# Additions of weight blocks in DRAM: placed under later products, and two blocks summed in place of three

## The chip, the cores and the metric

The kernel is one program on one core of a Trainium2 chip. The metric is the device time of an execution in microseconds, as the median of several runs. A core has five engines with an instruction queue each, which it works off in order: TensorE (PE, matrix products, with its weight loads as PEld), VectorE (DVE), ScalarE (ACT), GpSimd (POOL) and SyncE (SP). An engine whose next instruction waits for a semaphore does nothing of what stands behind it. Transfers are issued on the queues of SP, ACT and POOL and run beside the engines.

## The reference

One decoder block on 256 tokens of width 2048, in float32. What matters here are the stages and their order:

```python
u = rmsnorm(h, norm1_g[l])
proj = u @ w_in[l]                                   # 16896 columns
hq, hf, hi, hg, aq, ak, av, gate_a, gate_b = split(proj)
ya = hgrn2_branch(hq, hf, hi, hg, ...) @ w_proj_a[l]
yb = dilated_attention_branch(aq, ak, av) @ w_proj_b[l]
mix = sigmoid(gate_a) * ya + sigmoid(gate_b) * yb
h = h + mix @ w_out[l]
v = rmsnorm(h, norm2_g[l])
h = h + conv_ffn(v, w_up[l], conv_w[l], conv_b[l], w_down[l])
out = rmsnorm(h, norm_f_g)
```

The attention rotates q and k (`x1*cos - x2*sin`, `x2*cos + x1*sin`), and adds a mask to its scores.

## The kernel before

**The stream of weights.** All matrices are read once, as 300 units of 16 blocks of 128x128 (1 MB each), in the order in which they are multiplied: units 0 to 35 are the attention's columns, 36 to 99 HGRN's, 100 to 131 the gates', 132 to 167 the two projections and the output product, and from 168 on the up and down products of the feed-forward part, in eleven blocks b of 512 hidden columns. SP loads a unit into one of three tiles `raw` (L291). ScalarE rounds it to a high part (L368), VectorE forms the low part (L369), both called hl, and TensorE multiplies high and low parts separately (three matmuls for a product). `begin_unit` splits two units ahead and loads three ahead. So VectorE's hl operations are on the way of everything that TensorE does.

**Units of kind S.** In the up product most pairs of row blocks use seven products in place of eight (`PRODUCTS["S"]`), with sums of weight blocks. A unit holds b11, b21, b22 and b12, each 128x512. There are 49 such units. One of the sums is made in DRAM long before (`add_blocks`, L245): SP copies b12 into a DRAM tile q (L255), then POOL adds b11 (L256) and b22 (L257) to it with accumulating transfers. Each of the two waits on POOL until the one before it has landed. `begin_unit` spreads these 49 sums over the units from ADD_FROM = 20 on, ADD_SPAN = 140 units long. When the unit is loaded, three of its blocks come from the weights (L287) and the fourth is q (L288). `split_s` then makes the parts sa (b11, b21), se (b22 and the sum), sf (two more sums) and sg (one more), with three additions or subtractions on VectorE (L339, L340, L342).

**What else is on POOL.** The rotation of q and k needs the two halves of the head swapped, for which POOL issues two transfers each (L632, L633, tiles xs_q and xs_k). VectorE multiplies them with the sines (L638) and adds them (L640). POOL also loads the masks (L676, L677) and the table `lev` of HGRN's levels (L737), which ScalarE turns into seven masks `cu` (L741). While HGRN's first products (z0p) run, the attention's scores (sc), exponentials (L704), normalisation (L708) and transposes (tr, L715) are mixed in.

**PSUM banks.** The seven sums of a block lie in banks 1 to 7. `unfold` combines them: it reads p1 and p6 first (L597, L598), then p7 and p2 (L605, L607), p5 twice (L608, L609), p4 and p3 (L610, L611). The two down products of a block follow directly (tiles dn, L525 to L527), one with banks 1 and 6, the other with 4 and 5. A matmul into a bank waits until `unfold` has read it.

**What sets the order.** Apart from the first products and SP's additions, which are tied to a place, a scheduler in the compiler arranges each engine's instructions by its own estimate of times.

Of the kernel before, what the change touches and what calls it, by code (L numbers as in the profile page):

```python
# [11 lines left out]
F32 = mybir.dt.float32  # L12
# [3 lines left out]
ALU = mybir.AluOpType  # L16
AX = mybir.AxisListType

P = 128
# [12 lines left out]
FB = 4  # L32
# [19 lines left out]
def up_modes(b):  # L52

    return "PPPSSPSP" if b < 3 else UP_PAIRS
# [5 lines left out]
def up_order(b):  # L60


    return {0: (0, 1, 2, 5, 3, 7, 4, 6), 1: (0, 1, 2, 3, 5, 4, 6, 7), 2: (0, 1, 2, 3, 5, 4, 6, 7)}.get(b, tuple(range(KD // 2)))
# [66 lines left out]
NUNITS = len(stream_spec()[0]) // UNIT  # L130
MODES = stream_spec()[1]
ADDS = sum(mode == "S" for mode in MODES.values())
ADD_FROM, ADD_SPAN = 20, 140

# [49 lines left out]
def hybrid_block(ctx, tc, x_p, x_t, weights, g1, gf, params, c_rope, c_mask0, c_mask1, c_level, out):  # L186
    nc = tc.nc
    vec, act, pe = nc.vector, nc.scalar, nc.tensor
# [16 lines left out]
    def stage(name):  # L205
        return late["stage"].tile([P, 512], F32, tag="o2", name=name, bufs=6 if "pool" in late else STAGES - 2)
# [4 lines left out]
    def e4(shape, name):  # L211
        return sbe.tile([P] + list(shape), F32, tag="e4", name=name, bufs=4)
# [4 lines left out]
    def bank(i, name):  # L217
        return ps8.tile([P, 512], F32, tag=f"b{i}", name=name)

    def main_bank(name):  # L220
        turn[0] += 1
        return bank((turn[0] - 1) % 4, name)
# [20 lines left out]
    raws, splits, late = {}, {}, {}  # L243
    dram = ctx.enter_context(tc.tile_pool(name="dram", bufs=1, space=bass.MemoryType.DRAM))
    loaded, ready, to_add = [], {}, deque(sorted(u for u, mode in MODES.items() if mode == "S"))  # L245

    def add_blocks():

        if not to_add:
            return  # L250
        u = to_add.popleft()
        ready[u] = q = dram.tile([P, 512], F32, tag=f"q2_{u}", name=f"q2_{u}")
        b = [weights[u, :, i * 512 : (i + 1) * 512] for i in range(4)]
        with in_turn(loaded[-1]):
            nc.sync.dma_start(q, b[3])  # L255
        nc.gpsimd.dma_start(q, b[0], accum_op=ALU.add)  # L256
        nc.gpsimd.dma_start(q, b[2], accum_op=ALU.add)  # L257

    ring = [0]
    last = [None, None]  # L260
# [1 line left out]
    @contextmanager  # L262
    def in_turn(*instructions):

        with ExitStack() as stack:
            for i in instructions:
                stack.enter_context(tc.issue_after(i.ins))
            yield
# [44 lines left out]
    def two_parts(hi, lo, src):  # L313

        act.activation(hi, src, AF.Copy)  # L315
        vec.tensor_tensor(lo, src, hi.bitcast(F32), op=ALU.subtract)  # L316

    def pair_tile(name):

        more = late.get("pool")  # L320
        n = ring[0] % (6 if more else 4)
        ring[0] = (n + 1) if more else (n + 1) % 4
        pool, bufs = (wp, 4) if n < 4 else (more, 2)
        return pool.tile([P, 2, 1024], F32R, tag="pair", name=name, bufs=bufs)

    def split_s(u):

        r = raws[u].rearrange("p (b n) -> p b n", b=4)
        pool = late["pool"]

        def parts(name, src):
            t = pair_tile(name)
            hi, lo = t[:, 0].rearrange("p (b n) -> p b n", b=2), t[:, 1].rearrange("p (b n) -> p b n", b=2)
            two_parts(hi, lo, src)
            return [(hi[:, i], lo[:, i]) for i in range(2)]

        b11, b21 = parts(f"sa{u}", r[:, 0:2])
        b22, q2 = parts(f"se{u}", r[:, 2:4])
        vec.tensor_tensor(r[:, 0], r[:, 3], r[:, 0], op=ALU.subtract)  # L339
        vec.tensor_tensor(r[:, 1], r[:, 3], r[:, 1], op=ALU.add)  # L340
        q3, q4 = parts(f"sf{u}", r[:, 0:2])
        vec.tensor_tensor(r[:, 3], r[:, 3], r[:, 2], op=ALU.subtract)  # L342
        g = pool.tile([P, 2, 512], F32R, tag="sg", name=f"sg{u}", bufs=1)
        two_parts(g[:, 0], g[:, 1], r[:, 3])
        splits[u] = {"11": b11, "21": b21, "22": b22, "q3": q3, "q2": q2, "q4": q4, "q1": (g[:, 0], g[:, 1])}

    def split(u):
        if u >= NUNITS or u in splits:
# [36 lines left out]
    def pump(us):  # L385
        debt[0] += us
        while side and debt[0] > 0:
            try:
                debt[0] -= next(side[0])
            except StopIteration:  # L390
                side.popleft()
        if not side:
            debt[0] = min(debt[0], 0.0)

    def drain():
        while side:
            for _ in side[0]:
                pass
            side.popleft()
        debt[0] = 0.0  # L400

    def begin_unit(u):
        for v in range(u, u + LOOKAHEAD + 1):
            split(v)
        load(u + LOOKAHEAD + 1)
        pump(SIDE_US)
        if u >= ADD_FROM and (u - ADD_FROM) * ADDS // ADD_SPAN < ADDS:
            while len(to_add) > ADDS - 1 - (u - ADD_FROM) * ADDS // ADD_SPAN:
                add_blocks()
# [110 lines left out]
    def moving_step(pst, parts, k, k0, nk):  # L520

        hi, lo = next_tiles(4)
        for m in range(2):
            xh, xl = parts(k, m)
            pe.matmul(pst[m], xl, hi, start=(k == k0), stop=False)  # L525
            pe.matmul(pst[m], xh, hi, start=False, stop=False)  # L526
            pe.matmul(pst[m], xh, lo, start=False, stop=(k == k0 + nk - 1))  # L527

    def moving(parts, k0, nk, name, pst=None):

        pst = pst or [main_bank(f"{name}_{m}") for m in range(2)]
        for k in range(k0, k0 + nk):
            moving_step(pst, parts, k, k0, nk)
        return pst
# [2 lines left out]


    PRODUCTS = {
        "S": ((1, "a11", "11"), (2, "a12", "21"), (6, "x2", "q2"), (3, "x4", "22"), (7, "x3", "q3"), (4, "a22", "q4"), (5, "x1", "q1")),  # L540
        "P": (
            (2, "a11", "11"), (2, "a12", "21"), (4, "a21", "11"), (4, "a22", "21"),
            (5, "a21", "12"), (5, "a22", "22"), (3, "d1", "12"), (3, "d2", "22"),
# [32 lines left out]
    def sevenfold(ops, modes_of, order, name):  # L576

        sums = {i: late_bank(i, f"{name}_{i}") for i in range(1, 8)}
        left = {i: sum(p[0] == i for mode in modes_of for p in PRODUCTS[mode]) for i in sums}
        fresh = set(sums)  # L580
        for i in order:
            w = next_pair()
            for b, x, n in PRODUCTS[modes_of[i]]:
                (xh, xl), (wh, wl) = ops[i][x], w[n]
                left[b] -= 1
                pe.matmul(sums[b], xl, wh, start=b in fresh, stop=False)  # L586
                pe.matmul(sums[b], xh, wh, start=False, stop=False)  # L587
                pe.matmul(sums[b], xh, wl, start=False, stop=left[b] == 0)  # L588
                fresh.discard(b)
        return sums  # L590
# [269 lines left out]
    def four(name, by_half=False):  # L860

        t = e4([2, HG, P], name) if name[0] == "q" else w4([2, HG, P] if by_half else [HG, T], name)
        for h in range(HG):
            ps = stationary(x_pair, KD, f"{name}p{h}")
            if by_half:
                second = w1(f"{name}t{h}")
                act.activation(second, ps[:, T:], AF.Copy)
                vec.tensor_tensor(t[:, :, h], halves(ps[:, :T]), halves(second), op=ALU.add)
            else:
                summed(ps, t[:, h], f"{name}t{h}")  # L870
        if by_half:
            r = halves(rstd)[:, :, None, :].to_broadcast([P, 2, HG, P])
        else:
            r = rstd[:, None, :].to_broadcast([P, HG, T])
        vec.tensor_tensor(t, t, r, op=ALU.mult)
        return t
# [6 lines left out]
    for g in range(NGRP):  # L883
        z = four(f"z{g}", True)
        f = e4([2, HG, P], f"f{g}")
        act.activation(f, z, AF.Sigmoid)
        act.activation(z, z, AF.Sigmoid, scale=-1.0)
        for h in range(HG):
            i = g * HG + h
            vec.tensor_scalar(f[:, :, h], f[:, :, h], lb[:, 1, i : i + 1], lb[:, 0, i : i + 1], op0=ALU.mult, op1=ALU.add)  # L890
            vec.tensor_scalar(z[:, :, h], z[:, :, h], lb[:, 1, i : i + 1], None, op0=ALU.mult)
        q = four(f"q{g}", True)
# [4 lines left out]
        pst = moving(x_parts, 0, KD, f"gp{g}")  # L897
# [79 lines left out]
    for j in range(NJ):  # L977
        pst = moving(mix_parts, 0, KD, f"wo{j}")
# [23 lines left out]
    def late_bank(i, name):  # L1002
        return bank(place[i], name)
# [50 lines left out]
    for b in range(NBLK):  # L1054
        sums = sevenfold(hv, up_modes(b), up_order(b), f"up{b}")
        drain()
        side.append(hidden_side(b, sums))
        pump(0.0001)
        for j, b0, b1 in DOWN.get(b, ()):
            pst = moving(ff_parts, b0 * FB, (b1 - b0) * FB, f"dn{b}_{j}", [late_bank(i, f"dn{b}_{j}_{i}") for i in ((4, 5) if j % 2 else (1, 6))])  # L1060
            for m in range(2):
                if b == NBLK - 1:
                    vec.tensor_tensor(ht[j][:, m], ht[j][:, m], pst[m], op=ALU.add)
                else:
                    t = stage(f"dns{b}_{j}_{m}")
                    act.activation(t, pst[m], AF.Copy)  # L1066
                    nc.gpsimd.dma_start(ht[j][:, m], t, accum_op=ALU.add)  # L1067
# [9 lines left out]
    for m in range(2):  # L1077
# [16 lines left out]
        v, r, t = v3[:, mc], r3[:, mc], s3[:, mc]  # L1094
# [57 lines left out]
```

## Time and profile before

| what | us |
|---|---|
| runs: median (lowest to highest of 3) | 1750.25 (1747.96 to 1752.4) |
| the profiled execution | 1752.61 |
| its span, first to last instruction | 1750.8 |
| mean granted TensorE clock | 0.994 |

| stage by the trace, us from the start | PE busy | clock | DMA share |
|---|---|---|---|
| 100 to 150 | 50.00 of 50 | 1.00 | 0.74 |
| 150 to 200 | 48.55 of 50 | 1.00 | 0.83 |
| 200 to 250 | 32.47 of 50 | 0.83 | 0.57 |
| 400 to 500 | 100.00 of 100 | 1.00 | 0.70 |
| 1700 to 1751 | 42.50 of 51 | 0.97 | 0.28 |

In the rows of a profile "L369" is the line of the kernel, and "hl<-raw" the tiles written and read, without their numbers. A row of the timeline gives the start, the duration, and in brackets how long the engine had been idle before it and what ended that. The granted clock is the share of full speed that TensorE was allowed. A matmul's duration (0.39) overlaps the next one; the starts lie 0.23 apart.

### The profile page before, as it was taken

To read this page: it belongs to the slowest core of one execution; us is meant where nothing else is said; L and a number is where in the kernel's file an instruction comes from. 1 tells how busy PE (TensorE), PEld (TensorE's weight loads), DVE (VectorE), ACT (ScalarE), POOL (GpSimd) and SP (SyncE) were. 2 spreads that over 40 slices of the span, in tenths; PEclk is the share of its full clock that TensorE was granted. 3 is DMA by queue.
4 is the path that set the end of the run, shared out by engine and by line. 5 is a ranking of instruction groups with operands and counts; after the bars stand their busy time and mean duration, and the time that the engine had idled before them with its cause. 6 is when DMAs were issued, how large, how long until landed. Compare 5 with 4: busy or idle time off the path is not lost.

```text
span 1750.8 us, 21856 instructions
## 1 busy us (share of the span) xinstructions
PE 1720.1 (98%) x8325; PEld 1441.0 (82%) x8325; DVE 1299.6 (74%) x1562; ACT 1035.4 (59%) x1414; POOL 120.5 (7%) x159
## 2 busy tenths in 40 slices
PE   9999879999999999999999999999999999999998
PEld 7888768888888888888888888788888888888886
DVE  7665547586867766544565678899999989989986
ACT  6444346555555454544443667778777776776773
POOL 0001110000000010001010000000000000000000
PEclk9999989999999999999999999999999999999999
DMA  7668755767776776688887756656666566566562
GB/s 276 230 209 248 199 171 163 221 216 204 216 216 211 217 219 213 209 247 229 279 255 233 222 170 215 214 194 201 222 227 220 188 229 228 176 233 235 185 253 96
DMA packets 81785, 376.05 MB, mean 215 GB/s; under 512 B 9312, under 2 KB 9568, under 8 KB 49808
## 3 DMA queue, kind: packets, MB, share of 16 engines
q1 hardware_dynamic: 59616, 330.87, 52.7%
q0 software_dynamic: 20768, 40.38, 14.2%
q10 hardware_dynamic: 1296, 3.41, 0.5%
q8 instruction: 65, 1.06, 0.2%
q14 instruction: 40, 0.33, 0.1%
HBM read 359.94 MB, written 40.63 MB: 229 GB/s over the span
## 4 chain that ended last, share of the span: by engine, by line
PE 87%; issue 6%; DMA 4%; DVE 2%; ACT 1%; SPq 0%; POOL 0%; DVEq 0%; ACTq 0%; POOLq 0%
PE up L586 7%; PE up L588 7%; PE up L587 7%; PE dn L525 4%; PE dn L527 4%; PE dn L526 4%; PE egp L526 3%; PE egp L525 3%; PE egp L527 3%; DMA q<-weights 2%; PE aq L438 2%; PE ak L438 2%; PE gp L525 2%; PE wo L525 2%; PE gp L527 2%
## 5 line engine op out<-in xcount | busy, mean ns | idle before, releaser
L368 ACT ACTIVATE hl<-raw 128x1024 fp32r<-128x1024 f32 (+1 forms) x502 | 526.0, 1055 | 520.3 <-PE egp L527 79.4
L369 DVE TENSOR_TENSOR hl<-raw,hl 128x1024 fp32r<-128x1024 f32 (+1 forms) x502 | 605.5, 1219 | 303.9 <-ACT hl L368 301.8
L525 PE MATMUL dn<-hl,ff 128*128 128x512 f32 x320 | 127.2, 397 | 0.0
L527 PE MATMUL dn<-hl,ff 128*128 128x512 f32 x320 | 124.9, 390 | 0.0
L526 PE MATMUL dn<-hl,ff 128*128 128x512 f32 x320 | 124.7, 390 | 0.0
L525 PE MATMUL egp<-hl,xu 128*128 128x512 f32 x256 | 100.5, 393 | 0.0
L527 PE MATMUL egp<-hl,xu 128*128 128x512 f32 x256 | 99.8, 390 | 0.0
L526 PE MATMUL egp<-hl,xu 128*128 128x512 f32 x256 | 99.7, 389 | 0.0
L315 ACT ACTIVATE sf<-raw 128x1024 fp32r<-128x1024 f32 x49 | 52.3, 1067 | 69.3 <-DVE raw L340 69.0
L586 PE MATMUL up<-hl,hva 128*128 128x512 f32 x198 | 77.3, 390 | 0.0
L587 PE MATMUL up<-hl,hva 128*128 128x512 f32 x198 | 77.2, 390 | 0.0
L588 PE MATMUL up<-hl,hva 128*128 128x512 f32 x198 | 77.1, 389 | 0.0
L256 POOL DMA_DIRECT2D q<-weights x49 | 40.1, 818 | 501.4 <-DMA q<-weights 501.4
L1067 POOL DMA_DIRECT2D h<-dns x36 | 31.1, 917 | 617.8 <-ACT dns L1066 610.8
L527 PEld LDWEIGHTS dn<-hl,ff 128*128 128x128 f32 x320 | 60.1, 188 | 12.9
L525 PEld LDWEIGHTS dn<-hl,ff 128*128 128x128 f32 x320 | 60.1, 188 | 11.7
L526 PEld LDWEIGHTS dn<-hl,ff 128*128 128x128 f32 x320 | 60.2, 188 | 11.6
L438 PE MATMUL ak<-xu,hl 128*128 128x512 f32 x192 | 68.0, 399 | 0.0
L316 DVE TENSOR_TENSOR se<-raw,se 128x1024 fp32r<-128x1024 f32 x49 | 59.8, 1221 | 9.6 <-ACT se L315 9.6
L316 DVE TENSOR_TENSOR sf<-raw,sf 128x1024 fp32r<-128x1024 f32 x49 | 59.9, 1222 | 9.0 <-ACT sf L315 9.0
L316 DVE TENSOR_TENSOR sa<-raw,sa 128x1024 fp32r<-128x1024 f32 x49 | 59.8, 1221 | 4.5 <-ACT sa L315 3.7
L315 ACT ACTIVATE sa<-raw 128x1024 fp32r<-128x1024 f32 x49 | 52.0, 1062 | 14.6 <-PE up L588 6.6
(587 smaller groups left out, 4420.2 us busy)
## 6 DMA issues: line engine op xcount, KB each, us to landing
raw<-weights SPq DMA_DIRECT2D x249, 1024.0 KB, 5.3
raw<-weights SPq DMA_DIRECT2D x49, 768.0 KB, 4.3
q<-weights POOLq DMA_DIRECT2D x98, 256.0 KB, 6.4
q<-weights SPq DMA_DIRECT2D x49, 256.0 KB, 5.6
raw<-q SPq DMA_DIRECT2D x49, 256.0 KB, 4.6
h<-dns POOLq DMA_DIRECT2D x36, 256.0 KB, 3.8
h<-x_t ACTq DMA_DIRECT2D x4, 512.0 KB, 5.7
xt<-x_p SPq DMA_DIRECT2D x3, 512.0 KB, 10.0
```

What stands on the lines that cost most here:

```text
L256: nc.gpsimd.dma_start(q, b[0], accum_op=ALU.add)
L315: act.activation(hi, src, AF.Copy)
L316: vec.tensor_tensor(lo, src, hi.bitcast(F32), op=ALU.subtract)
L368: last[0] = act.activation(hi[:, q * w : (q + 1) * w], raw, AF.Copy)
L369: last[1] = vec.tensor_tensor(lo[:, q * w : (q + 1) * w], raw, hi[:, q * w : (q + 1) * w].bitcast(F32), op=ALU.subtract)
L438: pe.matmul(ps, hi, pair, start=(k == 0), stop=False, skip_group_check=True)
L525: pe.matmul(pst[m], xl, hi, start=(k == k0), stop=False)
L526: pe.matmul(pst[m], xh, hi, start=False, stop=False)
L527: pe.matmul(pst[m], xh, lo, start=False, stop=(k == k0 + nk - 1))
L586: pe.matmul(sums[b], xl, wh, start=b in fresh, stop=False)
L587: pe.matmul(sums[b], xh, wh, start=False, stop=False)
L588: pe.matmul(sums[b], xh, wl, start=False, stop=left[b] == 0)
```

## The change

Three things. The sums in DRAM begin at unit 44 in place of 20 and are spread over 120 units. Each adds b11 to b12 only; the sum with b22 is now made on VectorE, first of the three operations, in a tile q of its own. Which sum comes from DRAM thereby changes from q2 to q1, and with it the place of products 5 and 6 in the row of seven, and the banks of the down products.

```diff
-ADD_FROM, ADD_SPAN = 20, 140
+ADD_FROM, ADD_SPAN = 44, 120
...
-        ready[u] = q = dram.tile([P, 512], F32, tag=f"q2_{u}", name=f"q2_{u}")
+        ready[u] = q = dram.tile([P, 512], F32, tag=f"q1_{u}", name=f"q1_{u}")
         b = [weights[u, :, i * 512 : (i + 1) * 512] for i in range(4)]
         with in_turn(loaded[-1]):
             nc.sync.dma_start(q, b[3])
         nc.gpsimd.dma_start(q, b[0], accum_op=ALU.add)
-        nc.gpsimd.dma_start(q, b[2], accum_op=ALU.add)
...
         b11, b21 = parts(f"sa{u}", r[:, 0:2])
-        b22, q2 = parts(f"se{u}", r[:, 2:4])
-        vec.tensor_tensor(r[:, 0], r[:, 3], r[:, 0], op=ALU.subtract)
-        vec.tensor_tensor(r[:, 1], r[:, 3], r[:, 1], op=ALU.add)
+        q2 = pool.tile([P, 512], F32, tag="q", name=f"q{u}", bufs=1)
+        vec.tensor_tensor(q2, r[:, 2], r[:, 3], op=ALU.add)
+        b22, q1 = parts(f"se{u}", r[:, 2:4])
+        vec.tensor_tensor(r[:, 0], q2, r[:, 0], op=ALU.subtract)
+        vec.tensor_tensor(r[:, 1], q2, r[:, 1], op=ALU.add)
         q3, q4 = parts(f"sf{u}", r[:, 0:2])
-        vec.tensor_tensor(r[:, 3], r[:, 3], r[:, 2], op=ALU.subtract)
         g = pool.tile([P, 2, 512], F32R, tag="sg", name=f"sg{u}", bufs=1)
-        two_parts(g[:, 0], g[:, 1], r[:, 3])
+        two_parts(g[:, 0], g[:, 1], q2)
...
-        "S": ((1, "a11", "11"), (2, "a12", "21"), (6, "x2", "q2"), (3, "x4", "22"), (7, "x3", "q3"), (4, "a22", "q4"), (5, "x1", "q1")),
+        "S": ((1, "a11", "11"), (2, "a12", "21"), (5, "x1", "q1"), (3, "x4", "22"), (7, "x3", "q3"), (4, "a22", "q4"), (6, "x2", "q2")),
...
-[late_bank(i, f"dn{b}_{j}_{i}") for i in ((4, 5) if j % 2 else (1, 6))]
+[late_bank(i, f"dn{b}_{j}_{i}") for i in ((4, 6) if j % 2 else (1, 5))]
```

On POOL, at the end of the attention's products, stood before (q2_181 and the like are the sums in DRAM by their units, xs_k2 the last swap):

```order
L256 DMA q2_181_1634<-weights 128x512
L632 DMA xs_k2_1629<-akraw2_1430 64x1024
L633 DMA xs_k2_1629<-akraw2_1430 64x1024
L257 DMA q2_181_1634<-weights 128x512
L256 DMA q2_182_1735<-weights 128x512
L676 DMA mask0_1765<-c_mask0 128x384
L257 DMA q2_182_1735<-weights 128x512
L677 DMA mask1_1766<-c_mask1 128x768
L737 DMA lev_1771<-c_level 128x896
```

And there stands now:

```order
L632 DMA xs_k2_1613<-akraw2_1418 64x1024
L633 DMA xs_k2_1613<-akraw2_1418 64x1024
L676 DMA mask0_1741<-c_mask0 128x384
L677 DMA mask1_1742<-c_mask1 128x768
L737 DMA lev_1747<-c_level 128x896
L256 DMA q1_172_2347<-weights 128x512
L256 DMA q1_174_2482<-weights 128x512
```

Six units' additions stood ahead of the levels; the first of all 49 now stands behind them. On VectorE, at the last two swaps of k, the sum L640 also moved: it now follows L638 directly, with the hl that stood between them behind it.

On VectorE a unit of kind S in the feed-forward part (unit 238; raw238 is its tile) read before:

```order
L316 TENSOR_TENSOR sa238_10950<-raw238_10926,sa238_10950 128x1024
L316 TENSOR_TENSOR se238_10953<-raw238_10926,se238_10953 128x1024
L339 TENSOR_TENSOR raw238_10926<-raw238_10926 128x512
L340 TENSOR_TENSOR raw238_10926<-raw238_10926 128x512
L342 TENSOR_TENSOR raw238_10926<-raw238_10926 128x512
L316 TENSOR_TENSOR sf238_10958<-raw238_10926,sf238_10958 128x1024
L316 TENSOR_TENSOR sg238_10962<-raw238_10926,sg238_10962 128x512
```

And now (lines between the two places of the diff have moved up by one):

```order
L315 TENSOR_TENSOR sa238_10929<-raw238_10905,sa238_10929 128x1024
L338 TENSOR_TENSOR q238_10932<-raw238_10905 128x512
L315 TENSOR_TENSOR se238_10934<-raw238_10905,se238_10934 128x1024
L340 TENSOR_TENSOR raw238_10905<-q238_10932,raw238_10905 128x512
L341 TENSOR_TENSOR raw238_10905<-q238_10932,raw238_10905 128x512
L315 TENSOR_TENSOR sg238_10942<-q238_10932,sg238_10942 128x512
L315 TENSOR_TENSOR sf238_10939<-raw238_10905,sf238_10939 128x1024
```

The sum has moved ahead of se, and sg no longer reads the raw tile. In some other units L338 stands ahead of sa, or one hl of the unit before it.

On TensorE, at the end of block 6's up product (the third part of a name is the bank), stood before:

```order
L588 MATMUL up6_3_10783<-hl239_1_10991,hvd7_7899 128x512
L525 MATMUL dn6_2_1_11098<-hl240_0_11020,ff3_0_9794 128x512
L526 MATMUL dn6_2_1_11098<-hl240_0_11020,ff3_0_9794 128x512
L527 MATMUL dn6_2_1_11098<-hl240_0_11020,ff3_0_9794 128x512
L525 MATMUL dn6_2_6_11099<-hl240_0_11020,ff3_0_9794 128x512
```

And now:

```order
L588 MATMUL up6_3_10760<-hl239_1_10971,hvd7_7850 128x512
L525 MATMUL dn6_2_1_11078<-hl240_0_11000,ff3_0_9762 128x512
L526 MATMUL dn6_2_1_11078<-hl240_0_11000,ff3_0_9762 128x512
L527 MATMUL dn6_2_1_11078<-hl240_0_11000,ff3_0_9762 128x512
L525 MATMUL dn6_2_5_11079<-hl240_0_11000,ff3_0_9762 128x512
```

The first matmul into the second bank waits for another read of `unfold`. In other blocks the scheduler has pulled more matmuls into bank 1 ahead of the first into bank 5: eleven in blocks 2, 4 and 10, nine in block 3, six in block 5, three in blocks 6 to 9. In block 1 all of the first bank's and a bank of the second product come first. Behind block 0, which has no down product, 20 matmuls now stand ahead of the first into bank 5: 18 into bank 2, and two of unit 179's sg into bank 6, pulled ahead of two whole units. On VectorE stand until L609 there: L598, two hl around it, L605, L338 of unit 179, L608.

More of the change, by code (lines that the diff above doesn't have):

```diff
@@ L337, in split_s @@
         b11, b21 = parts(f"sa{u}", r[:, 0:2])
-        b22, q2 = parts(f"se{u}", r[:, 2:4])
-        vec.tensor_tensor(r[:, 0], r[:, 3], r[:, 0], op=ALU.subtract)
-        vec.tensor_tensor(r[:, 1], r[:, 3], r[:, 1], op=ALU.add)
+        q2 = pool.tile([P, 512], F32, tag="q", name=f"q{u}", bufs=1)
[3 more added lines that the diff above has]
+        vec.tensor_tensor(r[:, 1], q2, r[:, 1], op=ALU.add)
         q3, q4 = parts(f"sf{u}", r[:, 0:2])
-        vec.tensor_tensor(r[:, 3], r[:, 3], r[:, 2], op=ALU.subtract)
         g = pool.tile([P, 2, 512], F32R, tag="sg", name=f"sg{u}", bufs=1)
-        two_parts(g[:, 0], g[:, 1], r[:, 3])
-        splits[u] = {"11": b11, "21": b21, "22": b22, "q3": q3, "q2": q2, "q4": q4, "q1": (g[:, 0], g[:, 1])}
+        two_parts(g[:, 0], g[:, 1], q2)
+        splits[u] = {"11": b11, "21": b21, "22": b22, "q3": q3, "q1": q1, "q4": q4, "q2": (g[:, 0], g[:, 1])}
     def split(u):
@@ L1059, in hybrid_block @@
         for j, b0, b1 in DOWN.get(b, ()):
-            pst = moving(ff_parts, b0 * FB, (b1 - b0) * FB, f"dn{b}_{j}", [late_bank(i, f"dn{b}_{j}_{i}") for i in ((4, 5) if j % 2 else (1, 6))])
+            pst = moving(ff_parts, b0 * FB, (b1 - b0) * FB, f"dn{b}_{j}", [late_bank(i, f"dn{b}_{j}_{i}") for i in ((4, 6) if j % 2 else (1, 5))])
             for m in range(2):
```

## The prediction

> **What bounds the kernel now.** I read the engine totals first, then what TensorE waits for.
>
> ```profile
> PE 1720.1 (98%) x8325; PEld 1441.0 (82%) x8325; DVE 1299.6 (74%) x1562; ACT 1035.4 (59%) x1414; POOL 120.5 (7%) x159
> ```
>
> TensorE is busy for 1720.1 of 1750.8 us. A change that leaves the number of matmuls alone can win only the other 30.7 us, and what a low clock costs inside the busy time. The list of waits says where those are (line of the waiter, what it waited for, total, times, longest):
>
> ```profile
> PE tr L715 <- DVE sm L708: 13.0, 1, 13.0
> PE avp L527 <- DVE hl L369: 4.5, 1, 4.5
> PE ak L439 <- DVE hl L369: 1.4, 1, 1.4
> ...
> PE ub1t L1016 <- ACT ua1e L1024: 1.0, 1, 1.0
> ```
>
> The first three lie close together. The table of stretches (us; busy time of PE, PEld, DVE, ACT and POOL; granted clock; DMA share; GB/s) shows them, and what follows each:
>
> ```profile
> 182.00:188.00 6.00, 4.55 (x26) 3.71 (x25) 5.96 (x7) 1.81 (x3) 1.24 (x2) 1.00 0.59 100
> ...
> 212.00:216.00 4.00, 4.00 (x12) 3.14 (x12) 4.00 (x4) 0.22 (x1) 0.00 (x0) 0.62 0.37 68
> ...
> 230.00:243.40 13.40, 0.38 (x3) 0.07 (x2) 2.55 (x6) 6.50 (x12) 0.26 (x1) 0.70 0.33 82
> 243.40:250.00 6.60, 6.60 (x29) 6.07 (x30) 4.87 (x8) 1.82 (x3) 0.87 (x1) 0.56 0.60 209
> ```
>
> So 18.9 us of waiting lie between 182 and 244 us, at the end of the attention's products, and two stretches after them run at a clock of 0.62 and 0.56. What ends these waits is found on POOL, in order of time:
>
> ```profile
> 169.52 0.54 POOL L633 DMA_DIRECT2D xs_q<-aqraw  x1
> ...
> 198.57 0.81 POOL L256 DMA_DIRECT2D q<-weights  x1 [11.29 <-DMA q<-weights]
> 199.10 0.83 POOL L632 DMA_DIRECT2D xs_k<-akraw  x1
> 199.66 0.81 POOL L633 DMA_DIRECT2D xs_k<-akraw  x1
> ...
> 221.13 0.82 POOL L256 DMA_DIRECT2D q<-weights  x1 [11.65 <-DMA q<-weights]
> 221.68 0.88 POOL L676 DMA_DIRECT2D mask<-c_mask  x1
> 228.27 0.84 POOL L257 DMA_DIRECT2D q<-weights  x1 [5.72 <-DMA q<-weights]
> 228.81 0.90 POOL L677 DMA_DIRECT2D mask<-c_mask  x1
> 229.39 0.88 POOL L737 DMA_DIRECT2D lev<-c_level  x1
> ```
>
> POOL is a queue in order. An addition (L256, L257) waits there until the copy or addition before it has landed, and the rotation's swap (xs_k), the masks and the levels stand behind it. On the engines that want those transfers:
>
> ```profile
> 180.95 1.23 DVE L638 TENSOR_TENSOR xs_q<-xs_q,rope 128x1024 f32<-128x1024 f32 x1 [6.63 <-DMA xs_q<-aqraw]
> ...
> 192.59 0.42 DVE L451 TENSOR_TENSOR akraw<-ak,akt 128x256 f32<-128x256 f32 x1
> ...
> 206.70 0.39 PE L526 MATMUL avp<-hl,xu 128*128 128x512 f32 x1
> ...
> 209.19 1.23 DVE L638 TENSOR_TENSOR xs_k<-xs_k,rope 128x1024 f32<-128x1024 f32 x1 [11.07 <-DMA xs_k<-akraw]
> 210.33 1.22 DVE L369 TENSOR_TENSOR hl<-raw,hl 128x1024 fp32r<-128x1024 f32 x1
> ...
> 236.87 3.74 ACT L741 ACTIVATE cu<-lev 128x512 uint8<-128x512 f32 x7 [12.98 <-DMA lev<-c_level]
> ...
> 243.40 0.90 PE L715 MATMUL tr<-ident,sm 128*128 128x128 f32 x3 [13.02 <-DVE sm L708]
> ```
>
> VectorE is in order too: while it waits for xs_k, it splits no weights (hl), and TensorE runs dry. ScalarE waits for the levels with the exponential queued behind them, and TensorE's transposes wait for that.
>
> **The change, part by part.** By the order of the changed kernel POOL's rows from the swaps to the levels hold no addition; all 49 stand behind.
>
> *The swap of q (xs_q).* Its second half was issued at 169.52 and used at 180.95, with additions in flight. The landing times of the three xs_q, then of the three xs_k (least, median, most):
>
> ```profile
> DMA to landing us min/median/max: 5.0/7.6/11.3
> ```
> ```profile
> DMA to landing us min/median/max: 7.2/8.4/9.4
> ```
>
> At the median of 7.6 it lands at 177.1, 3.8 us sooner, more than the 1.4 us that TensorE waited. Bounds: 0 (it lands after 11.3 again) to **1.4**; I take 1.4.
>
> *The swap of k.* Its data are complete at 193.01 (192.59 + 0.42), so both halves go out by 193.6 instead of 199.66. With the longest landing, 9.4, it is there at 203.0, 6.2 us sooner. The new order puts the sum L640 ahead of the next hl, so three operations at 1.14 us (209.19 to 210.33) end at 206.4. TensorE's last matmul before the wait ends at 207.1. The **4.5** go whole, with 0.7 us to spare; bounds 0 to 4.5.
>
> *Masks and levels.* They now follow the swap directly, from about 194 us. The levels took 7.4 us (229.39 to about 236.8), so they land near 203. ScalarE asks for them at 223.89 (236.87 - 12.98), or some 6 us earlier once the waits before are gone: covered by over 10 us. From the first cast to the transposes stay 6.53 us (236.87 to 243.40); started at 223.89 they reach 230.42, and TensorE gets there at 230.38 (243.40 - 13.02). Next late is thus this chain itself, by under 0.1: **12.9** of 13.0.
>
> *The clock.* 4.0 us at 0.62 and 6.6 us at 0.56 lose 4.0 x 0.38 + 6.6 x 0.44 = 1.5 + 2.9 = **4.4** against full clock, and go with the waits; bounds 0 to 4.4.
>
> The Trainium skill, "TensorE: Matmul & The Clock Gate", Part 1, says that an idle window of about 3.4 us halves the clock, and that a busy one of the same length restores it. That would be two times 1.7 us, 3.4 in place of 4.4, and the forecast would be 1 us later. The trace agrees on when: 0.62 and 0.56 behind 4.5 and 13.0 us, but 1.00 in the stretch with the wait of 1.4.
>
> *The additions themselves.* Half of POOL's 98 transfers go; 43 of the 49 additions are already under later stages, where nothing waits:
>
> ```profile
> q<-weights POOLq DMA_DIRECT2D x98, 256.0 KB, 6.4
> ```
> ```profile
> 800.00:900.00 100.00, 100.00 (x451) 82.59 (x450) 54.92 (x55) 42.89 (x44) 10.52 (x13) 1.00 0.88 265
> ...
> 1100.00:1700.00 600.00, 598.71 (x2715) 494.71 (x2715) 547.26 (x633) 449.92 (x666) 32.23 (x38) 1.00 0.64 216
> ```
>
> At a DMA share of 0.88 TensorE is busy for 100.00 of 100.00 us. Per unit there were 0.35 copies with 0.70 additions, and there are 0.41 with 0.41: less traffic. Neither gain nor loss. On SP the 49 copies only shift among the loads.
>
> *The third operand on VectorE.* q2 = b22 + q1 (L338) takes the place of q1 = q2 - b22 (L342), on equal tiles:
>
> ```profile
> L342 DVE TENSOR_TENSOR raw<-raw x5: 681/691/692, 1050.2 to 1099.5; 128x512 f32<-128x512 f32 x5
> ```
>
> Count and length stay, so 0; VectorE's 52.7 idle us of 600 (the stretch above) cover a little more. It now comes before the split of se and wants the unit's second load; what if that is late is a rival. A raw tile comes free about two operations sooner: 0, as TensorE is full.
>
> *Bank 5 in place of bank 6.* The first down product (dn) of a block now needs bank 5, which VectorE reads late, in L609; bank 6 was read first. The first dn and L609 in two blocks:
>
> ```profile
> 1228.43 0.39 PE L525 MATMUL dn<-hl,ff 128*128 128x512 f32 x1
> ...
> 1230.29 0.74 DVE L609 SCALAR_TENSOR_TENSOR up3c<-up,rstd_r,up3c 128x512 f32<-128x512 f32 x1
> ```
> ```profile
> 1419.80 0.74 DVE L609 SCALAR_TENSOR_TENSOR up6c<-up,rstd_r,up6c 128x512 f32<-128x512 f32 x1
> ...
> 1419.87 0.39 PE L525 MATMUL dn<-hl,ff 128*128 128x512 f32 x1
> 1420.10 0.39 PE L526 MATMUL dn<-hl,ff 128*128 128x512 f32 x1
> ```
>
> Matmuls start 0.23 apart. In block 3 the bank comes free 2.60 us behind the first dn, and nine rows ahead of it cover 2.04: it costs 0.6. In block 6 it is 0.67 against three rows, 0.68: 0, or 0.1 with the hand-over. The order puts eleven rows ahead in blocks 2, 4 and 10, six in 5, three in 7 to 9; block 1 has more still. Taking block 6's 0.1 to 0.3 where three to six rows cover: 0.6 + 5 x 0.25, **1.8** in all. Bounds: 0 to 0.6 in each of nine, 5.4.
>
> *The end of block 0.* There p6 is now the last product. The order fills the gap with 20 matmuls (4.5 us) before bank 5 is asked for; VectorE's operations until then are five of about 0.69, as L342's, and one hl of 1.14: 4.6. I take **0.3**; bounds 0 and 2.6, two waits for a load as ScalarE has them further on (14.3 us over 11, the last row of the rivals).
>
> **Sum.** 1.4 + 4.5 + 12.9 + 4.4 = 23.2 won, 1.8 + 0.3 = 2.1 given back, net 21.1. The profiled execution took 1752.61 us (span 1750.8): 1731.5. It lies 2.4 above the median of the runs, 1750.25, to which the forecast belongs: **1729**.
>
> **The rivals.**
>
> *The swap of k is slow by itself.* Masks and levels, a megabyte, now follow it at once and may share its time. If it lands after 203.7, TensorE waits again, up to 4.5 with 1.5 of clock: 1735. For it: the 11.3 of one xs_q. Against: nothing but the weights' loads stands ahead of it, and the masks are behind it in its own queue.
>
> *Bank 5 binds.* One more hl (1.14) ahead of L609 in each of nine blocks is 10 to 11 us: 1740. Against it: both orders hold the same operations there; for it: three rows are little cover.
>
> *VectorE waits for the second load of an S unit (slower).* The place is L338, 43 times from 1100 to 1700 us, with the hl of other units queued behind it. VectorE has 52.7 us to spare, so waits of 1.2 us each are free; beyond that each costs, and from (52.7 + 21.1) / 43 = 1.7 us the kernel is slower than before. At 2.0 it is 86 - 53 = 33 lost, 1762. The nearest row, ScalarE's for loads in that stretch, is for it in size, but counts only 11:
>
> ```profile
> ACT hl L368 <- DMA raw<-weights: 14.3, 11, 1.9
> ```
>
> The earlier release of the raw tiles speaks against it.
>
> *The moved additions take the loads' time.* If each of the six from under the attention cost the loads its whole 6.4 us, 38 us would be lost: about 1767. The 100.00 at a share of 0.88 speaks against it. The Trainium skill, "DMA: Bandwidth & Descriptors", "Issuing engines are not separate DMA queues", says that transfers from all queues run on the same 16 engines and interleave, so moving to another time or queue makes no room by itself; no row here shows TensorE paying for it.
>
> *That the change does nothing* is excluded by POOL's order; that the waits have another cause is the first rival.
>
> **Chances.** Forecast, 1726 to 1733: 68%. Slow swap, 1733 to 1737: 12%. Bank 5, 1735 to 1745: 8%. VectorE waits: 4%, half within 0.3% and half above. Additions in the loads' way: 2%. Better (the 1.0 of ub1t gone, nothing given back, a fast run): 6%, 1722 to 1726. The range from 1724 to 1737 holds the first two and most of the last. A measurement can tell about 0.3% (5 us): faster 0.93, same 0.03 (with the top of the bank's case), slower 0.04.
>
> **What would show it.** Right: no wait of PE over 0.5 us before 300 us, a clock of 1.00 from 200 to 250, PE busy there for 50 of 50, xs_k issued as soon as akraw is done. Waits of dn on L609 below 0.6 in blocks 3 to 9. Wrong: L638 or the transposes still waited for, PE waiting for hl from 1100 us on, or L338 idle for a DMA.

## The result, and the profile after

| | before | changed |
|---|---|---|
| runs, median (lowest to highest), us | 1750.88 (1747.96 to 1752.4, 4 runs) | 1733.13 (1730.64 to 1734.78, 4 runs) |
| profiled execution, us | 1752.61 | 1732.29 |
| its span, us | 1750.8 | 1730.5 |
| mean granted clock | 0.994 | 0.998 |

The ratio is 0.9899, with a 95% interval of 0.9881 to 0.9918: 17.75 us by the medians, 20.3 by the two profiles. The forecast was 1729 with a range of 1724 to 1737.

The totals by engine, from the page of the changed kernel:

```profile
PE 1717.3 (99%) x8325; PEld 1436.1 (83%) x8325; DVE 1298.2 (75%) x1562; ACT 1036.0 (60%) x1414; POOL 81.1 (5%) x110
```

TensorE is busy for 2.8 us less in a span that is 20.3 us shorter, so the rest was idle time; POOL ran 49 instructions fewer. The waits of TensorE, all that the list shows (waiter, what it waited for, total, times, longest):

```profile
PE up L586 <- ACT sg L314: 1.7, 1, 1.7
PE warm L379 <- POOL c L235: 1.0, 1, 1.0
PE rstd_ps L469 <- DVE ssq L486: 0.5, 1, 0.5
PE avp L525 <- DVE xu L310: 0.4, 1, 0.4
PE dn L525 <- DVE up2c L609: 0.3, 1, 0.3
```

The 13.0, 4.5 and 1.4 us, and the 1.0 of ub1t, are gone; 1.7 and the 0.3 of dn are new. The 1.0 of `warm` belongs to the start of both kernels. The same stretches as before (busy time of PE, PEld, DVE, ACT and POOL; clock; DMA share; GB/s):

```profile
182.00:188.00 6.00, 6.00 (x36) 5.20 (x36) 3.70 (x4) 2.39 (x3) 0.00 (x0) 1.00 0.75 261
212.00:216.00 4.00, 4.00 (x25) 3.54 (x24) 1.38 (x3) 1.36 (x2) 0.00 (x0) 1.00 0.52 190
230.00:243.40 13.40, 13.40 (x85) 11.69 (x84) 9.55 (x18) 8.24 (x16) 0.00 (x0) 1.00 0.24 92
243.40:250.00 6.60, 6.60 (x49) 6.09 (x48) 5.25 (x9) 6.03 (x9) 0.00 (x0) 1.00 0.44 159
```

TensorE is full and at clock 1.00 wherever it waited. POOL in order of time:

```profile
168.85 0.51 POOL L632 DMA_DIRECT2D xs_q<-aqraw  x1 [43.37 <-DVE aqraw L451]
...
191.46 0.51 POOL L632 DMA_DIRECT2D xs_k<-akraw  x1 [21.59 <-DVE akraw L451]
191.96 0.52 POOL L633 DMA_DIRECT2D xs_k<-akraw  x1
...
193.56 0.55 POOL L737 DMA_DIRECT2D lev<-c_level  x1
```

The swap waits for its data (akraw) alone, and the levels go out 36 us earlier. What wanted them:

```profile
199.49 1.23 DVE L638 TENSOR_TENSOR xs_k<-xs_k,rope 128x1024 f32<-128x1024 f32 x1 [3.16 <-DMA xs_k<-akraw]
...
215.61 3.74 ACT L741 ACTIVATE cu<-lev 128x512 uint8<-128x512 f32 x7
...
222.14 0.55 PE L715 MATMUL tr<-ident,sm 128*128 128x128 f32 x3
```

ScalarE no longer waits for the levels. The transposes start at 222.14, where 243.40 stood.

How far the gain lasts is read from the starts of four groups of matmuls (first and last start in us): the first and the last product of the feed-forward part, and the transposes in blocks 3 and 10. Before, and changed:

```profile
L586 PE MATMUL up<-hl,hva x198: 388/389/476, 1045.1 to 1673.1; 128*128 128x512 f32 x198
...
L1016 PE MATMUL ua3t<-ident,up3c x8: 270/272/273, 1233.9 to 1240.1; 128*128 128x128 f32 x8
...
L1016 PE MATMUL ua10t<-ident,up10c x8: 270/272/273, 1680.6 to 1686.8; 128*128 128x128 f32 x8
...
L1088 PE MATMUL last<-hl,ff x24: 388/389/389, 1723.7 to 1742.1; 128*128 128x512 f32 x24
```

```profile
L586 PE MATMUL up<-hl,hva x198: 388/389/475, 1021.4 to 1651.7; 128*128 128x512 f32 x198
...
L1016 PE MATMUL ua3t<-ident,up3c x8: 270/272/273, 1212.0 to 1218.2; 128*128 128x128 f32 x8
...
L1016 PE MATMUL ua10t<-ident,up10c x8: 270/272/273, 1659.6 to 1665.8; 128*128 128x128 f32 x8
...
L1088 PE MATMUL last<-hl,ff x24: 388/389/389, 1702.8 to 1721.1; 128*128 128x512 f32 x24
```

The lead is 23.7 us at the first product (1045.1 - 1021.4), 21.9 in block 3, 21.0 in block 10 and at the last product, 20.3 at the end of the span. So 23.7 were won and 3.4 given back: 1.8 up to block 3, 0.9 from there to block 10, 0.7 behind the last product. The first loss has its place at the end of block 0. The timeline of the changed kernel there, with rows of VectorE, ScalarE and TensorE:

```profile
1053.02 1.23 DVE L369 TENSOR_TENSOR hl<-raw,hl 128x1024 fp32r<-128x1024 f32 x1 [1.14 <-ACT hl L368]
...
1055.89 0.74 DVE L605 SCALAR_TENSOR_TENSOR up0c<-up,rstd_s,up0c 128x512 f32<-128x512 f32 x1
...
1056.56 0.68 DVE L338 TENSOR_TENSOR q<-raw 128x512 f32<-128x512 f32 x1
...
1057.35 0.63 ACT L314 ACTIVATE sg<-q 128x512 fp32r<-128x512 f32 x1 [1.14 <-DVE q L338]
1057.82 0.74 DVE L609 SCALAR_TENSOR_TENSOR up0c<-up,rstd_r,up0c 128x512 f32<-128x512 f32 x1
...
1058.03 0.50 PE L586 MATMUL up<-sg,hvx 128*128 128x512 f32 x1 [1.68 <-ACT sg L314]
...
1058.61 0.19 PEld L586 LDWEIGHTS up<-hl,hvb 128*128 128x128 f32 x1 [0.28 <-DVE up0c L609]
```

The sum of unit 179 (L338) stands behind a read of `unfold` (L605). ScalarE splits it (sg), and two matmuls with sg stand on TensorE ahead of the first into bank 5 (the one with hvb). That one was late as well: L609 frees bank 5 at 1058.56, 0.5 us behind the start of the first sg matmul, and the load of its weights waits for it (last row). VectorE itself is behind there, since its hl at 1053.02 had waited 1.14 us for ScalarE.

### The profile page after: what moved, and what is told of

The parts are those of the page before. It is cut to its first block, busy times and chain, and to the rows that moved or that the text cites. A ratio compares the mean times of both kernels' runs of the same rounds, so it can differ in the third digit from the quotient of the medians.

```text
span 1730.5 us, 21724 instructions
## 1 busy us (share of the span) xinstructions
PE 1717.3 (99%) x8325; PEld 1436.1 (83%) x8325; DVE 1298.2 (75%) x1562; ACT 1036.0 (60%) x1414; POOL 81.1 (5%) x110
## 4 chain that ended last, share of the span: by engine, by line
PE 93%; DVE 3%; DMA 2%; ACT 1%; issue 1%; SPq 0%; DVEq 0%; ACTq 0%
PE up L586 7%; PE up L587 7%; PE up L588 7%; PE dn L525 4%; PE dn L527 4%; PE dn L526 4%; PE egp L526 3%; PE egp L525 3%; PE egp L527 3%; PE ak L438 3%; PE aq L438 2%; PE gp L527 2%; PE wo L526 2%; PE gp L525 2%; PE wo L525 2%; PE wo L527 2%
```

## The experiments

The theory: POOL's queue alone made the waits (additions cost nothing beside other work), and what was given back comes from the two-block sum's order of products. All spans are of the profiled executions; ratios are to the kernel before, run beside.

**Place and sum apart.** The kernel before with the new place, and the changed kernel with the old one:

```diff
-ADD_FROM, ADD_SPAN = 20, 140
+ADD_FROM, ADD_SPAN = 44, 120
```

> The kernel before, with only the place of the additions moved (from unit 44, 120 units long); every sum still takes two additions of 6.4 us, so twice as many run under HGRN's products as in the changed kernel. Theory (the place alone wins, the additions cost nothing where they now run, and what the changed kernel gave back comes from the two-block sum): the first product of the feed-forward part comes 23.7 us earlier than before, as in the changed kernel, and nothing is given back behind it, so the profiled span is 1750.8 - 23.7 = 1727.1, 3 us under the changed kernel. Rival (half the additions were needed for the gain): TensorE waits again between 250 and 950 us, and the span is not under the changed kernel's 1730.5. Rival two (the changed kernel's last loss lies in something else than the products' order): PE waits at the seam behind block 0 here too, and the span is 1729 to 1731.

Measured: 1729.43 us (1728.84 to 1729.51), ratio 0.987 [0.9855, 0.9885], span 1727.6. No wait of TensorE over 1.2 us. The first product of the feed-forward part comes 23.1 us earlier (at 1022.0), the last one 23.2 (1718.9): nothing is given back:

```profile
L586 PE MATMUL up<-hl,hva x198: 388/389/477, 1022.0 to 1649.8; 128*128 128x512 f32 x198
...
L1088 PE MATMUL last<-hl,ff x24: 388/389/390, 1700.5 to 1718.9; 128*128 128x512 f32 x24
```

The place alone wins all, and the 98 additions under HGRN's and later products cost TensorE nothing.

> The changed kernel with the additions back at their old place (from unit 20, 140 units long); two blocks are summed, one addition per unit. Theory (what holds the swap of k is the addition's wait for its copy, which waits on SP, so halving the additions does not free it; only the second addition ahead of the levels goes): the wait of 4.5 us stays, the levels go out at about 222.5 in place of 229.4, the transposes' wait of 13.0 shrinks to about 6, and with 2.7 us given back in the feed-forward part the span is 1750.8 - 7 - 1 + 2.7 = 1745 to 1747. Rival (fewer additions clear POOL's queue by themselves): all waits go, span near the changed kernel's 1730.5. Second rival (no part of the gain is theirs): 1753.

Measured: 1742.58 us, ratio 0.9946 [0.9934, 0.9959], span 1741.6. Its waits:

```profile
PE tr L715 <- DVE sm L708: 8.6, 1, 8.6
PE up L586 <- ACT sg L314: 2.0, 1, 2.0
```

and its POOL queue:

```profile
191.53 0.82 POOL L256 DMA_DIRECT2D q<-weights  x1 [14.41 <-DMA q<-weights]
192.07 0.84 POOL L632 DMA_DIRECT2D xs_k<-akraw  x1
192.62 0.81 POOL L633 DMA_DIRECT2D xs_k<-akraw  x1
213.24 0.86 POOL L256 DMA_DIRECT2D q<-weights  x1 [19.80 <-DMA q<-weights]
...
214.93 0.85 POOL L737 DMA_DIRECT2D lev<-c_level  x1
```

Half of the theory failed: with half the additions the queue had caught up, and the swap of k went out on time (192.07), so the 4.5 went as well. What stayed is the addition that waits for its copy (213.24), with the levels behind it. The first product of the feed-forward part comes 12.9 us earlier (at 1032.2), the last 9.9: 3.0 are given back, as in the changed kernel.

**The changed kernel again**, on the same chip as these.

> The changed kernel once more, as the yardstick for the others of this set on the same chip. If the distance of the two profiles (20.3 us of span) is the change's own and the 17.75 us between the medians so far were scatter, the median lies 19 to 21 us under the kernel before; if not, about 17.5.

Measured: 1731.97 us (1731.42 to 1732.87) against 1752.48, ratio 0.9886 [0.9872, 0.9899], 20.5 us: the distance of the profiles is the change's own. Its profile (span 1730.3) has a lead of 23.2 us at the first product of the feed-forward part, 22.2 in block 3 and 21.2 in block 10; the first profile had 23.7, 21.9 and 21.0. So such leads are good to about half a microsecond. The place alone (at most 1729.51) lies under every run of it.

**The tables or the swaps off POOL**, in the kernel before:

```diff
-    nc.gpsimd.dma_start(mask0, c_mask0)
-    nc.gpsimd.dma_start(mask1, c_mask1)
+    act.dma_start(mask0, c_mask0)
+    act.dma_start(mask1, c_mask1)
...
-    nc.gpsimd.dma_start(lev, ...)
+    act.dma_start(lev, ...)
```

> The kernel before, with the masks and the levels issued on ScalarE's queue in place of POOL's; additions and swaps stay. Theory (the transposes' wait comes from POOL's order alone): the wait of 13.0 and the low clock behind it (2.9) go, the waits of 1.4 and 4.5 for the swaps stay, span 1750.8 - 15.9 = 1735. Rival (the levels are late because the additions take the transfers' time, whichever queue issues them): the levels land after 224 us all the same and less than 5 us are won, span above 1745.

Measured: 1742.39 us, ratio 0.9953 [0.9936, 0.997], span 1740.9: between the two. The transposes still wait 4.6 us, the hl 4.4. ScalarE's queue is in order too:

```profile
216.31 0.69 ACT L620 ACTIVATE av<-avp,rst 128x512 f32<-128x512 f32 x1 [1.32 <-PE avp L527]
216.32 0.34 ACTq L676 DMA_DIRECT2D mask<-c_mask  x1
...
217.42 0.53 ACTq L737 DMA_DIRECT2D lev<-c_level  x1
...
227.95 3.75 ACT L741 ACTIVATE cu<-lev 128x512 uint8<-128x512 f32 x7 [5.59 <-DMA lev<-c_level]
```

The levels now stood behind an operation that waits for TensorE, and took 10.4 us to land.

```diff
-        nc.gpsimd.dma_start(xs[0:64], raw[64:128])
-        nc.gpsimd.dma_start(xs[64:128], raw[0:64])
+        act.dma_start(xs[0:64], raw[64:128])
+        act.dma_start(xs[64:128], raw[0:64])
```

> The kernel before, with the swaps of q and k issued on ScalarE's queue; additions, masks and levels stay on POOL. Theory A, as the terms of the prediction are added up (each wait by itself): 1.4 + 4.5 + 1.5 of clock = 7.4 won there; the levels still go out at 229.4, so the transposes' wait grows from 13.0 to about 20 and nothing is won, span 1749 to 1752. Theory B (a loop: VectorE's wait for the swap holds the raw tiles, these hold SP's next load, behind it stands the copy for the next addition, and that holds the levels on POOL): without the first wait the copy goes out at about 206 in place of 214, the levels at about 221, and the transposes' wait stays near 12 to 13, span 1742 to 1744.

Measured: 1744.13 us (1743.1 to 1747.85, the last one profiled), ratio 0.9972 [0.996, 0.9984], span 1746.1. The waits for the swaps are gone, the transposes wait 15.2. The copy for the addition went out on SP at 207.6, where it was 214.2 before, and the levels followed. SP before, then SP and POOL with the swaps on ScalarE's queue:

```profile
214.23 0.50 SPq L255 DMA_DIRECT2D q<-weights  x1
```
```profile
207.61 0.50 SPq L255 DMA_DIRECT2D q<-weights  x1
...
217.36 0.81 POOL L256 DMA_DIRECT2D q<-weights  x1 [10.35 <-DMA q<-weights]
...
223.78 0.88 POOL L257 DMA_DIRECT2D q<-weights  x1 [4.47 <-DMA q<-weights]
224.35 0.89 POOL L737 DMA_DIRECT2D lev<-c_level  x1
```

The levels go out 5 us earlier than before (229.39), so the loop of theory B exists, though in this profile the wait grew by 2.2 and took part of the win. The profile is that of the slowest of nine runs; the spans of the other eight, 1741.3 to 1743.1, lie near what theory B gave.

Both edits together:

> The kernel before, with swaps, masks and levels all on ScalarE's queue, and the additions where they were, under the attention's products. Theory (only POOL's order costs, the additions under the attention cost nothing): all waits before 300 us go, 23 us won, span about 1727.5, as with the place alone (1727.6). Rival (the additions also take the loads' time there): TensorE still waits for hl or the transposes between 150 and 250 us, span 1731 or more. A third outcome: ScalarE's own queue is held by the swaps' wait for akraw, a few us of waits for hl, 1729 to 1733.

Measured: 1739.35 us, ratio 0.9939 [0.992, 0.9958], span 1737.8; the transposes wait 8.1. The levels went out at 211.7, again behind L620, and took 13.8 us to land. Late issue, or additions that slow the landing: this could not tell them apart. So the tables were loaded earlier instead, ahead of the last group of q and k, on POOL (without and with the swaps on ScalarE's queue):

```diff
     for j in range(1, AG):
+        if j == AG - 1:
+            mask0, mask1 = w4([AG, P], "mask0"), w4([AG, T], "mask1")
+            nc.gpsimd.dma_start(mask0, c_mask0)
+            nc.gpsimd.dma_start(mask1, c_mask1)
+            NL = len(LEVELS)
+            lev = w4([NL, 2, 64], "lev")
+            nc.gpsimd.dma_start(lev, ...)
         aq.append(attention_in(j, "q"))
```

> The kernel before, with the masks and levels loaded a third of the attention earlier, on POOL; swaps and additions stay there too. Theory: the transposes' wait of 13.0 and its low clock (2.9) go whole, which the tables on ScalarE's queue could not show since they went out late there too; the waits for the swaps (1.4 and 4.5, with 1.5 of clock) stay, span 1735. Rival (the wait is not the tables' but the attention's chain being late behind the swap): 1740 to 1745, as with the tables on ScalarE's queue (1740.9).

Measured: 1737.11 us (1734.62, the profiled one, to 1739.05), ratio 0.9932 [0.9907, 0.9956], span 1732.9. The transposes' wait is gone, 3.5 us for hl stay. The profile is of the fastest of four runs, and its hl waited less than the 4.5 us of before; by the medians 13.5 us were won, where the theory has 15.9.

> The kernel before, with the masks and levels loaded a third of the attention earlier (written ahead of the last group of columns, still on POOL), and the swaps on ScalarE's queue; the additions stay under the attention's products, three blocks each. Theory (the additions cost only what stands behind them on POOL): no wait of TensorE over 1 us before 300 us, lead at the feed-forward part 22 to 23.7, span 1727.5 to 1729. Rival (they also slow other transfers there, as the tables' landing of 13.8 us in the last set suggests): TensorE still waits some 5 to 10 us between 150 and 250 us, span 1733 to 1738.

Measured: 1730.54 us (1728.89, the profiled one, to 1734.19), ratio 0.9893 [0.987, 0.9917], span 1727.1. Two stretches of it:

```profile
120.00:182.00 62.00, 62.00 (x325) 52.90 (x324) 35.65 (x35) 27.14 (x32) 8.28 (x11) 1.00 0.85 257
182.00:250.00 68.00, 67.87 (x380) 58.41 (x379) 44.20 (x65) 38.68 (x59) 6.77 (x9) 1.00 0.75 224
```

The three-block additions run under the attention as before, at DMA shares of 0.85 and 0.75, and TensorE is full. The levels landed in 8.6 us there, against 8.9 in the changed kernel, which has no addition near. So in this execution the additions took time from nothing but what stood behind them on POOL. It is the fastest of four: the others have spans 0.8, 2.5 and 5.3 us longer, while those of the place alone lie within 0.6. Without a trace of the longer ones it is not shown whether the additions under the attention cost something there; the old banks alone, run beside it with no addition under the attention, spread by 3.6 us as well.

**What was given back**, on the changed kernel. Product 6 ahead of 7 and 4, its split ahead of sf (in `split_s` the two lines of g move up behind L338); with the banks as changed, and as before:

```diff
-(5, "x1", "q1"), (3, "x4", "22"), (7, "x3", "q3"), (4, "a22", "q4"), (6, "x2", "q2")
+(5, "x1", "q1"), (3, "x4", "22"), (6, "x2", "q2"), (7, "x3", "q3"), (4, "a22", "q4")
```

> The changed kernel with product 6 moved ahead of 7 and 4 (sg split ahead of sf), but the down products' banks as changed (1 and 5, 4 and 6). Theory (the two losses are separate: 2.1 at the seam behind block 0, 1.1 to 1.4 by bank 5): the seam's wait for sg goes, the delays of the first dn on L609 stay, span 1728.3 to 1728.9, about 1 us over the version with both (1727.5). Rival (bank 5 is no loss of its own): 1727.5 as there.

> The changed kernel with product 6 moved ahead of products 7 and 4, its parts sg split ahead of sf, and the down products' banks as before (1 and 6, 4 and 5). TensorE's order then no longer holds two matmuls of unit 179's sg behind block 0, and the first pair of down products waits for a bank that is read first. Theory (the changed kernel lost about 2.1 us at that seam, by sg, and some 1.1 us by bank 5): both go, span 1727 to 1728. Rival (the seam has its price whatever the order, since VectorE is the late one there): PE waits 1 to 2 us for another operand at the seam, span 1729.5 to 1731. If only the banks matter: 1729.4.

And the old banks alone:

```diff
-[late_bank(i, f"dn{b}_{j}_{i}") for i in ((4, 6) if j % 2 else (1, 5))]
+[late_bank(i, f"dn{b}_{j}_{i}") for i in ((4, 5) if j % 2 else (1, 6))]
```

> The changed kernel with the down products' banks as before (1 and 6, 4 and 5), the products' order as changed. Theory (bank 5, read late in L609, costs about 1.1 to 1.4 us over the blocks, and the seam behind block 0 another 2.1 that stays here): span 1729.1 to 1729.4. Rival (with product 6 last, bank 6 is as late as bank 5): 1730.5, as the changed kernel.

Lengths of the stretches in us, from the same four groups of rows as above:

| kernel | first up product to block 3 | block 3 to 10 | last product to the end | span |
|---|---|---|---|---|
| before | 188.8 | 446.7 | 8.7 | 1750.8 |
| place only | 188.6 | 446.7 | 8.7 | 1727.6 |
| changed | 190.6 | 447.6 | 9.4 | 1730.5 |
| changed, second profile | 189.8 | 447.7 | 9.3 | 1730.3 |
| order of 6 | 188.5 | 448.8 | 9.4 | 1729.5 |
| order of 6, old banks | 187.9 | 447.3 | 9.4 | 1727.5 |
| old banks | 189.4 | 447.6 | 9.4 | 1729.0 |

By runs: order of 6, 1731.62 (ratio 0.9896 [0.9878, 0.9914]); with old banks, 1729.41 (0.9871 [0.9857, 0.9884]); old banks alone, 1730.65 (0.9894 [0.9873, 0.9916]). The order takes 2.1 off the first stretch, or 1.3 against the second profile: VectorE reads product 6 (L598) while TensorE is still at product 4, L338 stands behind all reads of `unfold`, and TensorE waits there for neither sg nor bank 5. With that order, bank 5 costs 1.5 between blocks 3 and 10, more than the theory had, so the span lies 0.6 above its range; one wait of it stands in the list (0.9 us, dn on L609 in block 7). Order and old banks together came out as the theory had it (1727.5). The old banks alone came within 0.1 us of theirs (1729.0), but not for its reason: with product 6 last they win nothing between blocks 3 and 10. There an up product of the next block waits, seven times, for the copies of the down products (old banks alone):

```profile
PEld up L586 <- ACT dns L1066: 1.7, 7, 0.2
```

With order of 6 and old banks this row is nearly the same (1.6, 7 times), so it does not tell the two apart, and why the old banks win only with that order stays open.

**Both kinds of edit together**: order of 6 with old banks, early tables, swaps on ScalarE's queue.

> The version with product 6 earlier and the banks as before (span 1727.5), and in it the masks and levels loaded a third of the attention earlier and the swaps on ScalarE's queue. In the run with additions under the attention these two together gave a lead of 24.9 us at the feed-forward part in place of 23.7. Theory (the 1.2 us come from tables and swaps and are free of the additions' place): span 1726.3, 21 us or more under the changed kernel's kernel before, about 1 us under the version it is made from. Rival (the 1.2 us were the scheduler's order with the additions there): 1727.5 as that version.

Measured: 1729.45 us, ratio 0.9883 [0.9865, 0.9901], span 1727.5: the rival. It is no faster than order of 6 with old banks (1729.41) or the place alone (1729.43), the best two, both under the changed kernel.

## Why the prediction was right, point by point

- **What bounds the kernel, and POOL's order as the cause: right.** Shown by the run with the place alone, and by the one with early tables and the swaps off POOL, which leaves all additions under the attention and in its profile still loses all these waits.
- **The terms before 300 us: 23.2 forecast, 23.7 measured.** The swap of k was issued at 191.96 in place of 193.6 and landed in 7.5 us, not 9.4; the transposes did not wait. The rival of a slow swap did not come.
- **The clock: 4.4 forecast.** The waits sum to 18.9, so 23.7 leaves 4.8 for it, and the 23.2 of the second profile 4.3. The rows were nearer than 3.4 from two times 1.7 (the last section says why).
- **The waits as separate terms: right in the sum, but not separate.** By separate terms the swaps alone should have won nothing, since the levels would have gone out no sooner (theory A); they won 4.7 us of span, 6.2 by the medians. The first wait had held the load, the load the copy, and the copy the levels. Early tables alone won 17.9 (13.5 by the medians), both 23.7 (20.1).
- **The additions: neither gain nor loss, right.** 98 of them cost no more than 49 (1727.6 against 1730.5). That half of them go was no part of the gain at the new place.
- **Bank 5: 1.8 forecast, 1.0 to 1.4 measured:** 0.47 in block 2 (a gap of 0.70 between starts 0.23 apart, below; the second profile has none) and 0.9 or 1.0 from block 3 to 10. That it is the bank's own cost holds only in part: the old banks lose as much there as long as product 6 is last.

```profile
1154.74 0.39 PE L526 MATMUL dn<-hl,ff 128*128 128x512 f32 x1
1155.44 0.50 PE L525 MATMUL dn<-hl,ff 128*128 128x512 f32 x1 [0.31 <-DVE up2c L609]
```

- **The end of block 0: 0.3 forecast, about 2 measured. This is the term that was mis-sized.** Compared at equal counts of matmuls in the traces, the lead over the kernel before falls there by 2.2 us in the changed kernel and by 1.9 in its second profile, by 0.7 to 0.8 with order of 6, and not at all with the place alone. The step set VectorE's 4.6 us of operations against a cover of 4.5. In the trace the cover starts at 1051.96 and L609 frees bank 5 at 1058.56, 6.6 us later: the sum has one hl where two stand, and no wait, where VectorE waited 1.14 us for ScalarE. 6.6 less 4.5 is the 2.1. The cover had a fault too: two of its 20 matmuls use sg of unit 179, whose sum (L338) stood in that same row of operations, and when the cover itself would be ready was not asked. But bank 5 came free later than sg, so by this trace TensorE would have waited about as long without these two; no run left just these two out. The range for the step (up to 2.6) held it.
- **ub1t and ua2t: not forecast.** Their waits of 1.0 and 0.3 are gone in the changed kernel. They return where three blocks are summed at the new place (1.1 and 0.2), so they go with the order of the two-block version, and paid for part of the end of block 0. That the net gain came so near the forecast (20.3 and 21.1 us of span) is therefore partly luck: these 1.3 us, and half a microsecond more before 300 us, made up for most of what the end of block 0 and the end of the kernel cost beyond the forecast.
- **VectorE at L338: the rival did not come.** It waited for the second load 5 times, 3.9 us in all, and 1.7 us in the longest (the list of VectorE's waits); TensorE waited for none of it beyond what is told above.
- **From span to median.** Against its own profile the forecast was 1731.5, and 1732.29 came. The 2.4 us taken off for the median were scatter of few runs: the changed kernel's median lies 0.84 above its own profiled execution. This was most of the 4.1 us by which 1729 missed 1733.13.

What also stays open: 0.7 us behind the last product. From there to the end it takes 8.7 us before and 9.4 in the changed kernel, and 8.7 to 9.4 in the other runs; the operations behind it start at the same distances, the last output transfers 4.0 us behind it in both. Nor is it settled why the levels took 13.8 us to land on ScalarE's queue.

## What to carry to other kernels

An addition in DRAM waits on its issuing queue for the copy ahead of it; whatever else is issued there inherits that wait, so look first at what stands behind it, and move either one. When a scheduler fills a gap with pulled-ahead work, add up all that stands ahead of what ends the gap, with that engine's own waits, and ask of the pulled-ahead work too when its operands are ready. Halving the additions won 9.2 us of span, moving them 23.2, and both together no more than that.

## What the runs showed of the hardware

The granted clock changes on a grid. The trace's own records of low stretches (the idle end of a run left out), and the waits of TensorE that they belong to:

```
kernel                      wait of PE, us   clock 0.5 for, us   in units of 3.413
tables early                 3.5              3.413               1
tables on ScalarE's queue    4.4              3.413               1
tables on ScalarE's queue    4.6              3.413               1
before                       4.5              3.413               1
swaps and tables on it       8.1              6.827               2
sums only                    8.6             10.240               3
before                      13.0             13.653               4
swaps on ScalarE's queue    15.2             17.067               5
```

Every stretch is a whole number of 3.413 us, and waits of 1.2 to 2.0 us made none. The Trainium skill, "TensorE: Matmul & The Clock Gate", Part 1, gives a free-running window of 3413 ns; the records agree. How much of a low stretch lies behind the wait depends on where the restart falls in the grid: about 3.4 us behind the 4.5, 5.9 behind the 13.0, whose row shows how long the half clock went on:

```profile
235.70:249.30 13.60, 5.90 (x24) 5.42 (x25) 5.89 (x9) 8.32 (x15) 0.63 (x1) 0.51 0.26 98
```

At half speed these cost 1.7 and 3.0 us, 4.7 together, close to the 4.8 or 4.3 that were won. Of the waits measured here, 3.5 us was thus the shortest that cost more than itself.
